# RG-LRU mixer of a two-layer trunk: another tile order, 1+a on ScalarE and GpSimd, and two interleaved output tiles

## The chip, the cores and the metric

The kernel runs on one core of one Trainium2 chip. The metric is the device time of one execution in microseconds. A profile of one execution lies beside it; its span goes from the first to the last instruction.

## What is computed

A trunk of two residual layers on x of 512 positions by 1024 channels, float32. Layer 0 mixes with pooling and block-sparse attention, layer 1 with a gated linear recurrence (RG-LRU); a gated convolutional FFN follows each. Only the mixer of layer 1 and the way out of it are touched here:

```python
def rglru_mixer(h, w_in, conv_w, conv_b, w_a, b_a, w_x, b_x, lam, w_out):   # h = rms_norm(x)
    gate, xr = jnp.split(h @ w_in, 2, axis=-1)                  # 1280 channels each: 10 tiles of 128
    xr = causal_dwconv(xr, conv_w, conv_b)                      # 4 taps
    r = sigmoid(xb @ w_a + b_a)                                 # xb: xr in 10 blocks of 128 channels
    i = sigmoid(xb @ w_x + b_x)
    a = exp(-RG_C * r * softplus(-lam))
    b = sqrt(1 - a**2) * (i * xr)
    hs = scan over positions of  hs[t] = a[t] * hs[t-1] + b[t]
    return (gelu(gate) * hs) @ w_out                            # added to x, then norm and FFN
```

## The kernel before, in words

Channels lie on the 128 partitions, the 512 positions along the free axis. A float32 product is made of three TensorE matmuls in fp32r (`mm3`): weights and activations are each split into a high and a low part, and high x high, high x low and low x high are summed in PSUM. The high part of an activation is a cast on ScalarE, the low part a subtraction on VectorE (`split_of`). Weights come by SyncE's DMA queue into three raw buffers; `convert` casts a chunk on ScalarE (line 195, `whi`), subtracts on VectorE (line 196, `wlo`) and keeps four converted chunks; `wnext` asks for the chunk in use and three ahead. The chunks of 512 columns for the gates have one buffer of their own in this stage (`shi`, `slo`).

The mixer's work for ten tiles is listed letter by letter in `RG_ORDER` (line 64):

- x: 24 matmuls of a branch tile (`xr`), times the norm's row factor (line 786, `z`), first tap on ScalarE (789), three taps on VectorE (791), high and low part (796, 797, `xrs`). The first x also asks for the norm's factor: two matmuls (`bc`), a root and a reciprocal (283).
- p: the tile's two gate products, three matmuls each (`gp`), a sigmoid for each (809), then i times xr on GpSimd (813) and a tanh for the root's argument (815).
- g: 24 matmuls of a gate tile (`gt`) and the row factor (756).
- e, q: exponentials (760) and roots (765) of all tiles so far, each with its own activation table.
- s: one VectorE instruction makes (1+a) times the root (770), GpSimd multiplies by i times xr (771), VectorE scans (772).
- o, y: gelu of the gate tile (775); product with the scan's result (779) and its split (230, 231), which gives `yh`, `yl`.

The scheduler orders each engine's instructions when the kernel is built, those traced first ahead of others that are ready; TensorE's matmuls are tied into the order of the letters within this stage (`in_order`, with `pe["on"]` true), and each engine works through its own list in order. After the letters, `down((5, 5), ...)` makes eight output tiles (`dn`), one after another, each from ten tiles of `yh`, `yl` (30 matmuls) with two weight chunks of 640 columns; the sum is added to `X[d]` (312) and goes into the next norm.

Of the kernel before, what the change touches and what calls it, by code (L numbers as in the profile page):

```python
# [17 lines left out]
P = 128  # L18
# [20 lines left out]
    _n += _w  # L39
NPA = _n  # L40

# Order of the first mixer: u/f = pooled projection now / as filler between attention steps, c = centre a window sum,
# v = value projection, m = split a pooled tile, a = attention.
MIX_ORDER = "u3 c3 u2 v m m f1 f0 a".split()
# Fillers of the attention loop: u = next projection group, m = split, p = pooled product, o = output product.
FILL_ORDER = "uuuuuuuuuuuuuuuuupmmpopp"
POOL_ORDER = (3, 2, 1, 0)
FILL_RATES = [float(c) for c in "1.6 1.95 1.45".split()]
# [8 lines left out]
CENTRE_AT = 5  # L57
V_BANKS = ("mm", "mm", "s", "av")
WARM = 20
# Order of the RG-LRU: x = branch tile, p = its gate products, g = gate tile, e = exps, q = roots, s = scan, o = gelu,  # L60
# y = output tile.
RG_ORDER = []
_c = dict.fromkeys("xpgeqsoy", 0)
for _kind in "xxgxpxpqxpgpgpeqsxsxxsssopyooxpxypygpgpqesssoosygsogyyogoyyggooyy":
    RG_ORDER.append((_kind, _c[_kind]))
    _c[_kind] += 1
RAW, WB, AHEAD = 3, 4, 3
# [3 lines left out]
def tile_trunk(ctx: ExitStack, tc: tile.TileContext, xT, par, fpar, w_v, w_q, w_k, w_u, w_pool, w_po, w_ao,  # L71
# [30 lines left out]
    def MM(name):  # L102
        ring.append(ring.pop(0))
        return PS(name, ring[-1])
# [51 lines left out]
    for kind, n in RG_ORDER:  # L156
# [4 lines left out]
                chunks.append((r_ax[n // 2], 4 * P))  # L161
        elif kind == "g":
            chunks.append((r_in[n], 1024))
    for d in range(KD):
        chunks.extend([(r_out[d][:, :5 * P], 5 * P), (r_out[d][:, 5 * P:], 5 * P)])
    ffn_chunks(f1_in, f1_out)
    ready = []
    used = [0]
# [30 lines left out]
    def wnext(n, ahead=AHEAD):  # L199
        while len(ready) < min(used[0] + 1 + ahead, len(chunks)):  # L200
            convert()
        hi, lo, got = ready[used[0]]
        assert got == n
        used[0] += 1
        return hi, lo
# [17 lines left out]
    def mm3(ps, sh, sl, mh, ml, start, stop):  # L223
        mmul(ps, lhsT=sh, rhs=mh, start=start, stop=False, skip_group_check=True)
        mmul(ps, lhsT=sh, rhs=ml, start=False, stop=False, skip_group_check=True)
        mmul(ps, lhsT=sl, rhs=mh, start=False, stop=stop, skip_group_check=True)
# [69 lines left out]
            mm3(ps, wh[:, c], wl[:, c], norm.xh[k], norm.xl[k], k == 0, k == KD - 1)  # L296
        return ps

    def down(parts, yh, yl, after, cuts=None):
        nk = len(yh)  # L300
        for d in range(KD):
            w = [wnext(n * P) for n in parts]
            spans = cuts if cuts and d == KD - 1 else [slice(0, S)]
            for t in spans:
                ps = MM("dn")
                k = 0
                for n, (wh, wl) in zip(parts, w):
                    for i in range(n):
                        c = slice(i * P, (i + 1) * P)
                        mm3(ps[:, t], wh[:, c], wl[:, c], yh[k][:, t], yl[k][:, t], k == 0, k == nk - 1)  # L310
                        k += 1
                nc.vector.tensor_tensor(X[d][:, t], ps[:, t], X[d][:, t], op=ALU.add)  # L312
                if len(spans) > 1:
                    after(d, t)
            if len(spans) == 1:
                after(d)

# [1 line left out]
    phase("mix0", qka=20, pm=4, hn=5, bias=1, lg=4)  # L319
    psum("ps0", mm=3, s=2, tr=2, av=1)  # L320
    warm = onesr.bitcast(BF16)
# [356 lines left out]
        g()  # L678
    ring[:] = ["mm", "s", "mm", "s", "mm", "av"]

# [1 line left out]
    def ffn(layer, norm, after, cuts=None):  # L682
        def conv(m):
            c0 = (layer * 2 * NF + m) * 4
# [30 lines left out]
    n1 = Norm("nm1")  # L715
    ffn(0, nf, n1.tile_done)

# [1 line left out]
    phase("mix1", z=2, a=3, xrs=6, i=2, h=10, gz=6, shi=1, slo=1, yy=20)  # L719
    lam = prm[:, PC["lam"]:PC["lam"] + RB]  # L720
    sc = [cst.tile([P, RB], F32, name=f"sc{i}") for i in range(5)]
# [30 lines left out]
    for kind, n in RG_ORDER:  # L752
        if kind == "g":
            ps = up_tile(n1, "gt")
            GZ[n] = T("gz")
            nc.vector.tensor_tensor(GZ[n], ps, n1.bc, op=ALU.mult)
            continue
        if kind == "e":
            while exped < len(HS):
                tabled("exp", nc.scalar.activation(R[exped], R[exped], AF.Exp, scale=c8[:, exped:exped + 1]))  # L760
                exped += 1
            continue
        if kind == "q":
            while rooted < len(HS):
                tabled("sqrt", nc.scalar.activation(HS[rooted], HS[rooted], AF.Sqrt))
                rooted += 1
            continue
        if kind == "s":
            h = HS[n]
            nc.vector.scalar_tensor_tensor(h, R[n], 1.0, h, op0=ALU.add, op1=ALU.mult)  # L770
            nc.gpsimd.tensor_tensor(h, h, BB[n], op=ALU.mult)
            nc.vector.tensor_tensor_scan(h, R[n], h, 0.0, op0=ALU.mult, op1=ALU.add)  # L772
            continue
        if kind == "o":
            tabled("gelu", nc.scalar.activation(GZ[n], GZ[n], AF.Gelu_apprx_tanh))
            continue
        if kind == "y":
            z = GZ[n]
            nc.vector.tensor_tensor(z, HS[n], z, op=ALU.mult)
            yh[n], yl[n] = split_of(z, None, T("yy", F32R), T("yy", F32R))  # L780
            continue
        if kind == "x":
            ps = up_tile(n1, "xr")
            bc = n1.bc
            z = T("z")
            nc.vector.tensor_tensor(z, ps, bc, op=ALU.mult)
            cw = [pc("rcw", 4 * n + i) for i in range(4)]
            a = T("a")
            nc.scalar.activation(a, z, AF.Identity, scale=cw[3], bias=pc("rcb", n))
            for sh in range(1, 4):  # L790
                ins = nc.vector.scalar_tensor_tensor(a[:, sh:], z[:, :S - sh], cw[3 - sh], a[:, sh:], op0=ALU.mult,  # L791
                                                     op1=ALU.add)
                if sh == 1:
                    behind(ins, now["conv"])
            hi, lo = T("xrs", F32R), T("xrs", F32R)
            nc.scalar.copy(hi, a)
            now["conv"] = nc.vector.tensor_sub(lo, a, f(hi))
            XC[n] = (a, hi, lo)
            continue
        a, xh, xl = XC[n]  # L800
        if n % 2 == 0:
            gwh, gwl = wnext(4 * P)
        gt = []
        for s in range(2):
            c = slice((2 * (n % 2) + s) * P, (2 * (n % 2) + s + 1) * P)
            gp = PS("gp", "tr")
            mm3(gp, gwh[:, c], gwl[:, c], xh, xl, True, True)
            o = T("yy" if s == 0 else "i")
            tabled("sig", nc.scalar.activation(o, gp, AF.Sigmoid, bias=pc("ba" if s == 0 else "bx", n)))
            gt.append(o)  # L810
        R[n] = gt[0]
        BB[n] = T("yy")
        nc.gpsimd.tensor_tensor(BB[n], gt[1], a, op=ALU.mult)
        HS[n] = T("h")
        tabled("sig", nc.scalar.activation(HS[n], R[n], AF.Tanh, scale=c4[:, n:n + 1]))
    pe["on"] = False
    nf1 = Norm("nf1")
    down((5, 5), yh, yl, nf1.tile_done)
    phase("ffn1", z=4, a=4, gg=2, y=2, yy=30)

    def store(d, t=slice(0, S)):
# [74 lines left out]
```

## Time and profile before

| what | value |
|---|---|
| median of 3 runs | 1108.43 us (1108.22 to 1109.06) |
| span of the profiled execution | 1106.8 us |
| TensorE busy | 1091.4 us (99%) |
| VectorE, ScalarE, GpSimd busy | 726.8, 514.6, 89.7 us |
| granted TensorE clock, mean | 0.997 |
| mixer of layer 1, first branch matmul to the last output tile | 553.5 to 743.8 us |

The execution takes 1.6 us more than its span in the median of the runs. A matmul of 512 columns shows 0.39 us, but the next one starts 0.227 us after it: 24 of them take 5.44 us in the chain of work. An instruction on VectorE of 128x512 shows 0.68 us while the next starts 0.60 us after it. The time between brackets in a timeline row is the engine's idle time before it and what ended it.

### The profile page before, as it was taken

To read this page: it belongs to the slowest core of one execution; us is meant where nothing else is said; L and a number is where in the kernel's file an instruction comes from. 1 tells how busy PE (TensorE), PEld (TensorE's weight loads), DVE (VectorE), ACT (ScalarE), POOL (GpSimd) and SP (SyncE) were. 2 spreads that over 40 slices of the span, in tenths; PEclk is the share of its full clock that TensorE was granted. 3 is DMA by queue.
4 is the path that set the end of the run, shared out by engine and by line. 5 is a ranking of instruction groups with operands and counts; after the bars stand their busy time and mean duration, and the time that the engine had idled before them with its cause. 6 is when DMAs were issued, how large, how long until landed. Compare 5 with 4: busy or idle time off the path is not lost.

```text
span 1106.8 us, 12775 instructions
## 1 busy us (share of the span) xinstructions
PE 1091.4 (99%) x4895; PEld 893.2 (81%) x4895; DVE 726.8 (66%) x1013; ACT 514.6 (46%) x749; POOL 89.7 (8%) x70
## 2 busy tenths in 40 slices
PE   8999999999999999999999899999999999999998
PEld 6887778888888888888888687788888888888887
DVE  7777867877753477764486979448777435777631
ACT  6556656544432344444458695444444323444320
POOL 4030002100000000000202323120000000000000
PEclk9999999999999999999999999999999999999999
DMA  6332112222223322223332131342322243332241
GB/s 223 129 95 87 58 39 71 102 95 96 72 82 111 117 96 98 94 73 91 113 113 105 48 101 48 99 136 95 102 97 78 79 119 116 96 95 84 72 137 51
DMA packets 35261, 105.40 MB, mean 95 GB/s; under 512 B 4096, under 2 KB 4992, under 8 KB 35200
## 3 DMA queue, kind: packets, MB, share of 16 engines
q1 hardware_dynamic: 34416, 103.48, 28.7%
q10 hardware_dynamic: 784, 1.11, 0.4%
q8 instruction: 38, 0.62, 0.2%
q14 instruction: 23, 0.19, 0.1%
HBM read 101.43 MB, written 2.10 MB: 94 GB/s over the span
## 4 chain that ended last, share of the span: by engine, by line
PE 90%; DVE 6%; ACT 2%; issue 1%; DMA 0%; POOL 0%; SPq 0%; DVEq 0%; POOLq 0%; ACTq 0%
PE up L218 43%; PE dn L218 26%; PE tk L218 5%; PE xr L218 2%; PE gt L218 2%; PE po L218 2%; PE u L218 2%; PE ao L218 2%; DVE h L772 1%; PE s L218 1%; DVE wlo L196 1%; PE tr L221 1%; PE gp L218 1%; DVE a L791 1%; DVE h L770 1%
## 5 line engine op out<-in xcount | busy, mean ns | idle before, releaser
L195 ACT CAST whi<-wraw 128x1024 fp32r<-128x1024 f32 (+3 forms) x225 | 202.5, 904 | 281.0 <-PE dn L218 154.2
L196 DVE TENSOR_TENSOR wlo<-wraw,whi 128x1024 fp32r<-128x1024 f32 (+3 forms) x225 | 238.9, 1065 | 114.2 <-ACT whi L195 111.6
L218 PE MATMUL up<-xl,whi 128*128 128x512 f32 x704 | 274.0, 389 | 0.0
L218 PE MATMUL up<-xh,whi 128*128 128x512 f32 x704 | 273.9, 389 | 0.0
L218 PE MATMUL up<-xh,wlo 128*128 128x512 f32 x704 | 273.9, 389 | 0.0
L218 PE MATMUL dn<-yy,whi 128*128 128x512 f32 (+1 forms) x886 | 269.2, 386 | 2.4 <-ACT yy L230 2.0
L218 PEld LDWEIGHTS dn<-yy,whi 128*128 128x128 f32 x886 | 165.8, 189 | 36.9 <-ACT yy L230 2.8
L218 PE MATMUL dn<-yy,wlo 128*128 128x512 f32 (+1 forms) x443 | 170.7, 385 | 0.0
L218 PEld LDWEIGHTS up<-xl,whi 128*128 128x128 f32 x704 | 132.2, 188 | 27.9 <-DVE xl L234 0.5
L218 PEld LDWEIGHTS up<-xh,whi 128*128 128x128 f32 x704 | 132.2, 188 | 27.4
L218 PEld LDWEIGHTS up<-xh,wlo 128*128 128x128 f32 x704 | 132.2, 188 | 27.2
L693 DVE SCALAR_TENSOR_TENSOR a<-z,fprm,a 128x510 f32<-128x510 f32 (+1 forms) x176 | 131.1, 748 | 4.2 <-ACT a L691 1.1
L689 DVE TENSOR_TENSOR z<-up,rbc 128x512 f32<-128x512 f32 x88 | 60.5, 688 | 89.1 <-PE up L218 89.1
L218 PEld LDWEIGHTS dn<-yy,wlo 128*128 128x128 f32 x443 | 83.6, 189 | 16.4
L260 POOL TENSOR_TENSOR ss<-ss,sq 128x512 f32<-128x512 f32 x28 | 41.3, 1475 | 494.1 <-ACT sq L259 493.6
L230 ACT CAST yy<-y 128x512 fp32r<-128x512 f32 x44 | 27.3, 621 | 112.1 <-DVE y L707 112.1
L312 DVE TENSOR_TENSOR x<-dn,x 128x512 f32<-128x512 f32 (+1 forms) x41 | 27.8, 679 | 73.9 <-PE dn L218 73.9
L691 ACT ACTIVATE a<-z,fprm 128x512 f32<-128x512 f32 x88 | 71.4, 814 | 3.8 <-DVE z L689 3.2
L704 ACT ACTIVATE gg<-a 128x512 f32<-128x512 f32 x44 | 27.8, 632 | 81.1 <-DVE a L693 81.0
L231 DVE TENSOR_TENSOR yy<-y,yy 128x512 fp32r<-128x512 f32 x44 | 30.5, 692 | 28.9 <-ACT yy L230 28.9
L218 PE MATMUL tk<-wlo,xh 128*128 128x512 f32 x96 | 37.7, 392 | 1.9 <-DVE wlo L196 1.9
L218 PE MATMUL tk<-whi,xh 128*128 128x512 f32 x96 | 37.9, 400 | 1.2 <-ACT whi L195 1.2
(177 smaller groups left out, 1229.5 us busy)
## 6 DMA issues: line engine op xcount, KB each, us to landing
wraw<-in_dram SPq DMA_DIRECT2D x131, 512.0 KB, 3.3
wraw<-in_dram SPq DMA_DIRECT2D x48, 320.0 KB, 2.8
wraw<-in_dram SPq DMA_DIRECT2D x32, 384.0 KB, 3.0
x<-in_dram SPq DMA_DIRECT2D x8, 256.0 KB, 5.9
out_dram<-x SPq DMA_DIRECT2D x7, 256.0 KB, 2.0
wraw<-in_dram SPq DMA_DIRECT2D x6, 256.0 KB, 2.7
qka<-qka ACTq DMA_DIRECT2D x8, 128.0 KB, 2.6
wraw<-in_dram SPq DMA_DIRECT2D x4, 128.0 KB, 3.8
```

The source lines that it names most:

```text
L195: nc.scalar.copy(hi[:, c], raw[:, c])
L196: nc.vector.tensor_tensor(lo[:, c], raw[:, c], f(hi[:, c]), op=ALU.subtract)
L218: in_order(nc.tensor.matmul(*a, **k))
L221: in_order(nc.tensor.transpose(*a))
L230: nc.scalar.copy(hi, src)
L231: nc.vector.tensor_sub(lo, src, f(hi))
L260: nc.gpsimd.tensor_tensor(self.ss, self.ss, sq, op=ALU.add)
L312: nc.vector.tensor_tensor(X[d][:, t], ps[:, t], X[d][:, t], op=ALU.add)
L689: nc.vector.tensor_tensor(z, ps, bc, op=ALU.mult)
L691: nc.scalar.activation(a, z, AF.Identity, scale=cw[2], bias=cw[3])
L693: nc.vector.scalar_tensor_tensor(a[:, sh:], z[:, :S - sh], w, a[:, sh:], op0=ALU.mult, op1=ALU.add)
L704: nc.scalar.activation(gg, g, AF.Gelu_apprx_tanh)
```

## The change

`RG_ORDER` gets another string: four p stand among the first x, the first g comes after the first e and q, and later letters alternate. In step s the VectorE instruction of line 770 goes; ScalarE writes 1+a into a tile of the pool `i` (two buffers, shared with the gate i), GpSimd multiplies it into i times xr, GpSimd multiplies the root by that, and the scan follows. In `down`, the mixer's call sets `paired`: the first two output tiles take their first five inputs one after the other, then their last five; the weight chunks are ordered to suit. Comment lines go.

```diff
-for _kind in "xxgxpxpqxpgpgpeqsxsxxsssopyooxpxypygpgpqesssoosygsogyyogoyyggooyy":
+for _kind in "xxpxpxpxpxpeqgssxpssgsxpooyygxpoygxpoygpeqgssoygssoygsoygoygoyoy":
...
-    for d in range(KD):
-        chunks.extend([(r_out[d][:, :5 * P], 5 * P), (r_out[d][:, 5 * P:], 5 * P)])
+    halves = [slice(0, 5 * P), slice(5 * P, 10 * P)]
+    chunks += [(r_out[d][:, c], 5 * P) for c in halves for d in range(2)]
+    chunks += [(r_out[d][:, c], 5 * P) for d in range(2, KD) for c in halves]
...
-    def down(parts, yh, yl, after, cuts=None):
+    def down(parts, yh, yl, after, cuts=None, paired=False):
         nk = len(yh)
-        for d in range(KD):
+        if paired:
+            ps = [MM("dn") for _ in range(2)]
+            k0 = 0
+            for n in parts:
+                for d in range(2):
+                    wh, wl = wnext(n * P)
+                    for i in range(n):
+                        c = slice(i * P, (i + 1) * P)
+                        k = k0 + i
+                        mm3(ps[d], wh[:, c], wl[:, c], yh[k], yl[k], k == 0, k == nk - 1)
+                k0 += n
+            for d in range(2):
+                nc.vector.tensor_tensor(X[d], ps[d], X[d], op=ALU.add)
+                after(d)
+        for d in range(2 if paired else 0, KD):
...
             h = HS[n]
-            nc.vector.scalar_tensor_tensor(h, R[n], 1.0, h, op0=ALU.add, op1=ALU.mult)
+            up1 = T("i")
+            nc.scalar.activation(up1, R[n], AF.Identity, bias=ones)
+            nc.gpsimd.tensor_tensor(BB[n], up1, BB[n], op=ALU.mult)
             nc.gpsimd.tensor_tensor(h, h, BB[n], op=ALU.mult)
             nc.vector.tensor_tensor_scan(h, R[n], h, 0.0, op0=ALU.mult, op1=ALU.add)
...
-    down((5, 5), yh, yl, nf1.tile_done)
+    down((5, 5), yh, yl, nf1.tile_done, paired=True)
```

## Rows read from the trace of the kernel before

**Rows 1.** Page, busy time of the engines, share of the span, instructions.

```profile
PE 1091.4 (99%) x4895; PEld 893.2 (81%) x4895; DVE 726.8 (66%) x1013; ACT 514.6 (46%) x749; POOL 89.7 (8%) x70
```

**Rows 2.** Stretches: start:end, length, busy us (instructions) by engine, clock, DMA share, GB/s.

```profile
553.50:604.20 50.70, 50.70 (x226) 41.85 (x225) 39.23 (x44) 32.21 (x44) 6.91 (x5) 1.00 0.31 108
604.20:655.30 51.10, 47.27 (x199) 38.07 (x198) 46.37 (x52) 39.60 (x55) 17.22 (x10) 0.97 0.23 77
655.30:683.90 28.60, 27.36 (x122) 22.32 (x121) 21.79 (x24) 18.29 (x27) 10.54 (x6) 1.00 0.15 42
683.90:698.00 14.10, 11.67 (x41) 8.52 (x40) 11.41 (x17) 7.55 (x13) 0.00 (x0) 0.88 0.39 114
```

**Rows 3.** TensorE's waits from 550 to 760: total us, times, longest.

```profile
PE gp L218 <- ACT xrs L796: 3.2, 1, 3.2
PE dn L218 <- ACT yy L230: 2.0, 1, 2.0
PE gt L218 <- DVE wlo L196: 1.2, 1, 1.2
```

**Rows 4.** Chain of work: start us, length us, what.

```profile
564.90 5.44 PE gt L218 x24
...
575.78 1.36 PE gp L218 x6
```

**Rows 5.** VectorE's timeline at the mixer's start: start us, length us, instruction.

```profile
561.00 3.34 DVE L283 RECIPROCAL rbc<-ss 128x512 f32<-128x512 f32 x1
...
565.80 1.22 DVE L196 TENSOR_TENSOR wlo<-wraw,whi 128x1024 fp32r<-128x1024 f32 x1
566.94 2.31 DVE L791 SCALAR_TENSOR_TENSOR a<-z,prm,a 128x511 f32<-128x511 f32 x3
570.00 0.69 DVE L797 TENSOR_TENSOR xrs<-a,xrs 128x512 fp32r<-128x512 f32 x1 [0.74 <-ACT xrs L796]
```

**Rows 6.** ScalarE's timeline at the mixer's start.

```profile
565.67 1.52 ACT L789 ACTIVATE a<-z,prm 128x512 f32<-128x512 f32 x2
569.35 0.62 ACT L796 CAST xrs<-a 128x512 fp32r<-128x512 f32 x1 [2.16 <-DVE a L791]
```

**Rows 7.** Stretch right after TensorE's longest wait, columns as in Rows 2.

```profile
625.00:630.00 5.00, 5.00 (x16) 3.91 (x17) 5.00 (x7) 3.68 (x6) 0.00 (x0) 0.66 0.20 52
```

**Rows 8.** VectorE's timeline during the second five scans.

```profile
667.74 0.66 DVE L770 SCALAR_TENSOR_TENSOR h<-yy,h 128x512 f32<-128x512 f32 x1
668.32 1.21 DVE L772 TENSOR_TENSOR_SCAN h<-yy,h 128x512 f32<-128x512 f32 x1
669.46 1.71 DVE L770 SCALAR_TENSOR_TENSOR h<-yy,h 128x512 f32<-128x512 f32 x1
```

**Rows 9.** GpSimd's timeline: one product early, one during the second five scans.

```profile
580.00 1.29 POOL L813 TENSOR_TENSOR yy<-i,a 128x512 f32<-128x512 f32 x1 [22.48 <-ACT i L809]
...
668.54 2.07 POOL L771 TENSOR_TENSOR h<-h,yy 128x512 f32<-128x512 f32 x1 [1.81 <-DVE h L770]
```

**Rows 10.** VectorE's groups from 604.2 to 655.3: busy us, mean ns, idle before.

```profile
L196 DVE TENSOR_TENSOR wlo<-wraw,whi 128x1024 fp32r<-128x1024 f32 x7 | 9.5, 1369 | 0.2 <-ACT whi L195 0.2
...
L779 DVE TENSOR_TENSOR gz<-h,gz 128x512 f32<-128x512 f32 x3 | 2.0, 677 | 0.0
L756 DVE TENSOR_TENSOR gz<-gt,rbc 128x512 f32<-128x512 f32 x2 | 1.4, 678 | 0.0
```

**Rows 11.** Stretch of the second five scans and their products, columns as in Rows 2.

```profile
663.00:693.80 30.80, 27.16 (x116) 21.11 (x114) 28.19 (x34) 16.23 (x25) 9.08 (x5) 1.00 0.17 52
```

**Rows 12.** ScalarE's timeline after the last gate products.

```profile
656.23 0.71 ACT L815 ACTIVATE h<-yy,c 128x512 f32<-128x512 f32 x1
656.96 1.28 ACT L765 ACT_TABLE_LOAD   x1
658.26 2.71 ACT L765 ACTIVATE h<-h 128x512 f32<-128x512 f32 x5
660.98 1.28 ACT L760 ACT_TABLE_LOAD   x1
662.27 3.18 ACT L760 ACTIVATE yy<-yy,c 128x512 f32<-128x512 f32 x5
```

**Rows 13.** VectorE's timeline, low part of the last product y.

```profile
693.08 0.69 DVE L231 TENSOR_TENSOR yy<-gz,yy 128x512 fp32r<-128x512 f32 x1 [0.68 <-ACT yy L230]
```

## The prediction

> **What bounds the kernel now.** I read the page first, for the engine that is full: TensorE is busy for 99% of the span [rows 1], so a change pays only where it takes away time in which TensorE waits or runs slowly, or costs by making such time. Then the stretches of the mixer of layer 1, to see how much of that there is. Twenty-four matmuls take 5.44 us and the six of a gate pair 1.36 us [rows 4], so one matmul is 5.44/24 = 0.227 us. The first stretch holds eight 24-matmul tiles, five gate pairs and the two norm matmuls: 8 x 5.44 + 5 x 1.36 + 0.48 = 50.8 us in 50.7: nothing is lost. The second holds seven tiles and five pairs, 44.9 us in 51.1: 6.2 lost. The third holds five gate tiles, 27.2 in 28.6: 1.4 lost. The fourth holds 41 matmuls, 9.3 in 14.1: 4.8 lost [rows 2]. In all 12.4 us; no order of this stage can give back more.
>
> The waits say which instruction ends the loss: gate products wait 3.2 us for a high part of a branch tile, an output tile 2.0 us for the high part of a product y, a gate tile 1.2 us for a weight's low part [rows 3]. The rest of the 12.4 is slow running: after the longest wait the granted clock was 0.66 in 625 to 630, that is part of the stretch at 1.2 GHz and part at 2.4 [rows 7]. All three releasers hang on VectorE, or on ScalarE fed by VectorE. VectorE is busy for 46.4 of 51.1 us in the second stretch [rows 2] and 28.2 of 30.8 us from the second block of scans to the last y [rows 11]. So the mixer's bound is VectorE's queue, and how it stands against TensorE's order.
>
> VectorE's busy time hides a second user. A scan alone takes 1.21 us and line 770 alone 0.66; the next line 770, started at 669.46, took 1.71, ending at 671.17 [rows 8]. GpSimd's product began at 668.54, took 2.07 where it needs 1.29 alone, and ended at 670.61 [rows 9], 0.56 us before VectorE's ended. GpSimd stood still while the scan ran, and VectorE while GpSimd ran: with operands in SBUF the two take turns, and a GpSimd product costs VectorE up to 1.29 us, 1.05 in this pair (1.71 - 0.66).
>
> **The change part by part.** *The opening.* Before, the first gate products start at 575.78, after a gate tile and a third branch tile that fill 564.90 to 575.78 [rows 4]. Now "xxp" puts them at 564.90, and the matmul order is tied to the letters. Their input is the first branch tile's split: reciprocal until 564.34, first tap at 565.67, a weight's low part at 565.80, three taps from 566.94 to 569.25, cast from 569.35 to 569.97, low part from 570.00 to about 570.6 [rows 5, 6]. Nothing in the change makes this chain earlier: the reciprocal follows the last output tile of the FFN, and converted weight chunks are released by the same matmuls as before. So TensorE stands still from 564.90 to about 570.0 (5.1 us), makes one matmul and waits for the low part (0.5 us more). If the taps went ahead of the weight's low part (1.13 us) it would be 4.0 and 0.5. Then the clock: from the 3.2 us wait I take its price as the 6.2 us lost there less 3.2 and less about 1.5 us of second waits and slow gate products: 1.5 us; here 0.5 to 1.7. I take 5.6 + 1.2 = 6.8 us (bounds 4.5 to 7.5).
>
> *The pairs p1 to p4.* Each waits for a split whose tile ended one pair and one tile earlier: 1.36 + 5.44 = 6.8 us. The chain is row factor 0.6, first tap 0.8, three taps 2.3, cast 0.7, low part 0.6, and a GpSimd product in between 1.29 [rows 5, 6, 9]: 6.3 us, 7.4 if a weight's low part stands in front. So 0 to 0.6 us for each of three: 1 us in all (0 to 3).
>
> *From p4 to p9.* TensorE has now nine tiles and five pairs here, 9 x 5.44 + 5 x 1.36 = 55.8 us. Against the second stretch of before, VectorE has two more weight chunks (+2 x 1.2), two more gate tiles and one more y (about +1.3 each) [rows 10], and five line-770 instructions fewer (-5 x 0.66 [rows 8]): 46.4 + 5.0 - 3.3 = 48.1 us. GpSimd has five products more; a product adds between 0.8 us (if part of it falls into VectorE's idle time; an estimate from the 46.4 us, which are 8 us above what its 52 instructions take undisturbed, for ten products) and 1.29: 4.0 to 6.5. With the 4.7 us of idle of that stretch [rows 2] it comes to 56.8 to 59.2, against 55.8. x6 to x8 each have a gate tile between them and their p, so the lag shows at p9 alone. I take 2 us (0 to 6). ScalarE's ten additions of 0.76 each (its nearest row is the first tap, two in 1.52 [rows 6]) and one more table load of 1.28 [rows 12] find room, since it is busy for 39.6 of 51.1 us [rows 2]; without that room they would add up to 5 us here, because casts queue behind them.
>
> *After p9.* Count from the end of p9, 655.3 before. Before, tanh ends 1.6 us after it, and roots and exponentials with two loads end 10.1 us after it, while line 770 starts already at 663.0, +7.7 [rows 11, 12]. Now the addition comes behind both blocks on ScalarE: +10.1 + 0.8 = +10.9 until GpSimd can begin, and two GpSimd products stand ahead of each scan. VectorE's work from there: the 30.8 us of before [rows 11], less 5 x 0.66, less one y that now comes before p9 (1.3), plus five GpSimd products (4.0 to 6.5): 30.2 to 32.7. The last y is thus ready at +41.1 to +43.6; before it was at 693.8 [rows 13], +38.5. What TensorE can do meanwhile: five gate tiles, 27.2, and then in the paired order twice five inputs (30 matmuls, 6.8 us) and four more (2.7): it needs the last y at +36.7. One tile alone would need it at 27.2 + 9 x 0.68 = +33.3; the pairing gives 3.4 us. Left: 4.4 to 6.9 us. I take the low end and a clock loss of 1.0, 5.4 us (0 to 9; nothing if additions get ahead of roots, and TensorE fills the wait with a third output tile).
>
> The sum: 6.8 + 1 + 2 + 5.4 = 15.2 us lost in place of 12.4: +2.8 us on the profiled execution, 1106.8 + 2.8 = 1109.6 of span, and with the 1.6 us between span and median 1111.2 us. Moved DMAs are costed at nothing: SyncE's queue brings the same chunks at 108 GB/s and less in these stretches [rows 2], in the order of use; if a load came late it would cost one chunk's wait, as 1.2 us in [rows 3].
>
> By the Trainium skill, "SBUF — State Buffer", section "SBUF: two separate sides", the shared pair of ports is locked against GpSimd only by a VectorE instruction with two SBUF inputs or one in a two-port mode. No row here has a GpSimd product beside a multiplication out of PSUM, so no run shows it yet; by that rule the row factors of lines 756 and 786 would run beside GpSimd, which is the third rival.
>
> **The rivals.** *Faster, through slack.* The order gathers the recurrence's first half early and leaves gate tiles, which are cheap for VectorE (0.68 us each [rows 10] against some 4.5 for a branch tile), as filler. If that keeps every later split ahead of TensorE and the last y comes by +36.7, only the opening is lost: 6.8, perhaps 8 with a small wait. Then 12.4 - 8 to 12.4 - 6.8 = 4.4 to 5.6 us faster, about 1103.5. For it: p5 to p8 have 12 us of slack. Against it: VectorE and GpSimd together have more to do than before in both later stretches, and were full. It decides at +36.7 us after p9.
>
> *Worse, through two buffers.* The additions share two buffers with the gate i. If ScalarE stands at an addition whose buffer GpSimd still reads, casts queue behind it, and with them matmuls. With every GpSimd product at 1.29 and the queue's waits the upper bounds hold: 7 + 2 + 5 + 9 = 23 lost, +10.6: about 1119. For it: two GpSimd products for each scan; against: ScalarE has idle time.
>
> *Row factors beside GpSimd.* Nine row factors of 0.6 between p4 and p9 and four after p9 run while GpSimd works. That takes the 2 us of the middle away and 2.4 of the end: 15.2 - 4.4 = 10.8 lost, 1.6 us less than before: 1106.8. It needs them to fall together with products, which two lists in order don't promise.
>
> **How the numbers follow.** About 0.2% (2.2 us) is what a measurement of this kernel can tell from no change. My forecast, 1111.2 (own range 1108.5 to 1117), gets 0.50; faster through slack 0.25; row factors beside GpSimd 0.15; two buffers 0.10. Faster: 0.25. Slower: 0.10 and 0.42 of the forecast's 0.50. Same: the 0.15 and the forecast's lower edge, 0.08: 0.23. The range takes in the fast case and the slow one but for their tails: 1103 to 1119.
>
> **What would show it.** Right: TensorE idle for some 5 us before the first gate products, released by the first branch tile's split, with a clock below 1 soon after; small waits or none at p5 to p8; GpSimd twice as busy in the scans, VectorE instructions there over 1.6 us; the first scan of the second half 13 us after p9 instead of 10.2, and an output-tile matmul waiting for a late y. Wrong: the first pair not waiting (then the 6.8 goes, and it is faster), TensorE without a wait after p9, or waits for ScalarE's additions in the middle.

## The result, and the profile after

| | before | after |
|---|---|---|
| median | 1108.45 us (1108.22 to 1109.06) | 1126.49 us (1126.0 to 1126.88) |
| span of the profiled execution | 1106.8 us | 1124.4 us |
| granted TensorE clock, mean | 0.997 | 0.989 |

The ratio is 1.016 (95% interval 1.0145 to 1.0174): 18.0 us slower. The prediction was 1111.2 (1103 to 1119). It had the direction and missed the size: the loss is over six times the forecast's 2.8 us.

In after, most lines of before stand one line later up to the function `down`, and 15 to 17 lines later in the mixer: matmuls are L219, a weight's low part L197, scans L789, the two GpSimd products L787 and L788, the addition 1+a L786, the taps L808, the split of a branch tile L813 and L814. In the other kernels the numbers shift by a few lines; the names of the tiles tell which instruction it is.

The page of after, busy time of the engines, which answers to [rows 1]:

```profile
PE 1098.2 (98%) x4895; PEld 896.8 (80%) x4895; DVE 726.5 (65%) x1003; ACT 522.4 (46%) x760; POOL 102.6 (9%) x80
```

TensorE has the same 4895 matmuls and no longer fills the span. VectorE lost ten instructions and is as busy as before (726.5 against 726.8); GpSimd gained ten products and 12.9 us.

The stretches of after, cut where p4, p9 and the mixer's last output tile end (start:end, length, busy us and instructions of PE, PEld, DVE, ACT, POOL, then clock, DMA share, GB/s); the first two answer to the first two of [rows 2], and the last two lines are short stretches behind two waits, as [rows 7]:

```profile
553.50:603.60 50.10, 44.33 (x178) 34.47 (x177) 36.90 (x40) 27.64 (x38) 7.01 (x5) 0.93 0.25 85
603.60:672.30 68.70, 59.55 (x248) 47.48 (x247) 52.89 (x53) 49.11 (x67) 23.37 (x15) 0.93 0.25 78
672.30:761.40 89.10, 84.03 (x362) 69.06 (x361) 49.48 (x58) 48.52 (x71) 25.39 (x17) 0.96 0.30 86
570.00:575.00 5.00, 4.21 (x9) 3.13 (x10) 3.45 (x6) 3.81 (x6) 0.00 (x0) 0.50 0.12 48
699.40:712.00 12.60, 7.53 (x24) 5.74 (x23) 12.59 (x15) 4.89 (x8) 4.83 (x3) 0.73 0.21 57
```

With the prediction's 0.227 us a matmul (24-matmul tile 5.44, gate pair 1.36, the norm's two 0.48) the work needs 39.9, 55.8 and 81.6 us in these three stretches: six tiles and five pairs; nine tiles and five pairs; five gate tiles and eight output tiles of 30 matmuls. So 10.2, 12.9 and 7.5 us are lost, 30.6 in all (each to some 0.2 us). Cut at the same events, before loses 0, 6.2 and 6.9 (743.76 - 655.3 - 81.6): 13.1. The difference, 17.5, is within 0.1 us what the span grew by, 17.6. These three numbers are the measure for every experiment below.

TensorE's waits of after, 550 to 775 (engine, line, waited for: total us, times, longest), against [rows 3]:

```profile
PE gp L219 <- ACT xrs L813: 8.4, 3, 5.1
PE gt L219 <- DVE wlo L197: 5.4, 1, 5.4
PE dn L219 <- DVE wlo L197: 5.1, 1, 5.1
PE gp L219 <- DVE xrs L814: 0.9, 4, 0.2
```

The long ones in TensorE's timeline (in brackets the wait before the instruction and what ended it): the opening, two in the middle, one among the output tiles.

```profile
570.79 1.52 PE L219 MATMUL gp<-xrs,whi 128*128 128x512 f32 x2 [5.10 <-ACT xrs L813]
...
629.30 0.50 PE L219 MATMUL gp<-xrs,shi 128*128 128x512 f32 x1 [2.45 <-ACT xrs L813]
...
638.03 0.80 PE L219 MATMUL gt<-xh,wlo 128*128 128x512 f32 x1 [5.44 <-DVE wlo L197]
...
705.05 0.80 PE L219 MATMUL dn<-yy,wlo 128*128 128x512 f32 x1 [5.07 <-DVE wlo L197]
```

The first was forecast (5.1 us). The two longest of the others wait for the low part of a weight, which has nothing to do with the recurrence but for standing in VectorE's list. Its timeline in the first block of scans shows behind what:

```profile
618.32 2.30 DVE L789 TENSOR_TENSOR_SCAN h<-yy,h 128x512 f32<-128x512 f32 x1 [2.99 <-POOL h L788]
...
624.41 4.18 DVE L808 SCALAR_TENSOR_TENSOR a<-z,prm,a 128x511 f32<-128x511 f32 x3
...
633.57 2.27 DVE L789 TENSOR_TENSOR_SCAN h<-yy,h 128x512 f32<-128x512 f32 x1 [2.47 <-POOL h L788]
635.77 2.21 DVE L197 TENSOR_TENSOR wlo<-wraw,whi 128x1024 fp32r<-128x1024 f32 x1
```

and GpSimd's timeline beside it:

```profile
629.95 2.24 POOL L787 TENSOR_TENSOR yy<-i,yy 128x512 f32<-128x512 f32 x1 [2.68 <-ACT i L786]
632.26 1.27 POOL L788 TENSOR_TENSOR h<-h,yy 128x512 f32<-128x512 f32 x1
633.50 1.26 POOL L787 TENSOR_TENSOR yy<-i,yy 128x512 f32<-128x512 f32 x1
634.84 2.06 POOL L788 TENSOR_TENSOR h<-h,yy 128x512 f32<-128x512 f32 x1
```

Read the two together from 632.26. The product of L788 ends at 633.53, and the scan that needs it starts at 633.57, after VectorE had stood idle for 2.47 us. The next GpSimd product (633.50 to 634.76) falls on the scan, which takes 2.27 us in place of 1.21 [rows 8]. Behind it the weight's low part starts at 635.77 and meets the next product (634.84 to 636.90): 2.21 us in place of 1.22 [rows 5]. It ends at 637.98, and TensorE goes on at 638.03 after 5.44 us. The low part had no other work in front of it than a scan; the scan had two GpSimd products in front of it. The three taps at 624.41 show the same stretching: 4.18 us, against 2.31 [rows 5].

### The profile page after: what moved, and what is told of

It is laid out like the page before. It is cut to its first block, busy times and chain, and to the rows that moved or that the text cites. A ratio compares the mean times of both kernels' runs of the same rounds, so it can differ in the third digit from the quotient of the medians.

```text
span 1124.4 us, 12782 instructions
## 1 busy us (share of the span) xinstructions
PE 1098.2 (98%) x4895; PEld 896.8 (80%) x4895; DVE 726.5 (65%) x1003; ACT 522.4 (46%) x760; POOL 102.6 (9%) x80
## 4 chain that ended last, share of the span: by engine, by line
PE 88%; DVE 4%; ACT 4%; issue 1%; POOL 1%; DMA 0%; SPq 0%; ACTq 0%; POOLq 0%; DVEq 0%
PE up L219 43%; PE dn L219 26%; PE tk L219 5%; PE xr L219 2%; PE u L219 2%; PE po L219 2%; PE ao L219 2%; DVE a L808 2%; PE s L219 1%; PE gt L219 1%; DVE wlo L197 1%; PE tr L222 1%; PE av L219 1%; PE gp L219 1%; POOL yy L787 1%
## 5 line engine op out<-in xcount | busy, mean ns | idle before, releaser
L196 ACT CAST whi<-wraw 128x1024 fp32r<-128x1024 f32 (+4 forms) x226 | 203.2, 903 | 279.7 <-PE dn L219 153.8
L197 DVE TENSOR_TENSOR wlo<-wraw,whi 128x1024 fp32r<-128x1024 f32 (+4 forms) x226 | 240.3, 1067 | 109.8 <-ACT whi L196 107.2
L219 PE MATMUL up<-xl,whi 128*128 128x512 f32 x704 | 274.0, 389 | 0.0
L219 PE MATMUL up<-xh,whi 128*128 128x512 f32 x704 | 273.9, 389 | 0.0
L219 PE MATMUL up<-xh,wlo 128*128 128x512 f32 x704 | 273.9, 389 | 0.0
L219 PE MATMUL dn<-yy,whi 128*128 128x512 f32 (+1 forms) x886 | 268.6, 385 | 0.0
L219 PEld LDWEIGHTS dn<-yy,whi 128*128 128x128 f32 x886 | 166.1, 189 | 33.3
L219 PE MATMUL dn<-yy,wlo 128*128 128x512 f32 (+1 forms) x443 | 171.1, 386 | 5.1 <-DVE wlo L197 5.1
L219 PEld LDWEIGHTS up<-xl,whi 128*128 128x128 f32 x704 | 132.2, 188 | 28.1 <-DVE xl L235 0.5
L219 PEld LDWEIGHTS up<-xh,wlo 128*128 128x128 f32 x704 | 132.2, 188 | 27.3
L219 PEld LDWEIGHTS up<-xh,whi 128*128 128x128 f32 x704 | 132.2, 188 | 27.2
L219 PEld LDWEIGHTS dn<-yy,wlo 128*128 128x128 f32 x443 | 83.8, 189 | 22.0 <-DVE wlo L197 5.5
L219 PE MATMUL tk<-whi,xh 128*128 128x512 f32 x96 | 38.8, 410 | 0.6 <-ACT whi L196 0.6
L219 PE MATMUL tk<-wlo,xh 128*128 128x512 f32 x96 | 38.1, 397 | 0.9 <-DVE wlo L197 0.9
```

Source lines behind the costliest of these rows:

```text
L196: nc.scalar.copy(hi[:, c], raw[:, c])
L197: nc.vector.tensor_tensor(lo[:, c], raw[:, c], f(hi[:, c]), op=ALU.subtract)
L219: in_order(nc.tensor.matmul(*a, **k))
```

## The experiments

Each experiment is one edit of before or of after. "Lost" means the three numbers above: opening to the end of p4, to the end of p9, to the end of the mixer. A difference with a sign is against runs of before taken beside it (medians 1109.31, 1109.20 and 1108.73 us in three sets of runs); "less than after" compares medians of different sets. The lost numbers are those of the one profiled execution, which lies up to 1.7 us from its kernel's median. Six kernels give every engine the same list up to the end of p4 (after, and below the letters alone, 1+a back on VectorE, the product on VectorE, the scans set apart and the scans late), and they lose 8.8 to 10.2 us there; so 1 us or so between two lost numbers says nothing.

### Each part of the change alone

Three kernels take one part each into before. The order of the letters:

```diff
-for _kind in "xxgxpxpqxpgpgpeqsxsxxsssopyooxpxypygpgpqesssoosygsogyyogoyyggooyy":
+for _kind in "xxpxpxpxpxpeqgssxpssgsxpooyygxpoygxpoygpeqgssoygssoygsoygoygoyoy":
```

> The kernel before with the new string of letters alone; 1+a stays on VectorE, output tiles one after another. Theory A (the two-product step is what makes scans stand at the head of VectorE's list, with weights' low parts behind them): only the opening's loss of about 9 us is new, and the rest loses about as before, so 1113 to 1118. Theory B (the letters alone make the waits): 1122 or more, with the 5.4 us wait of a gate tile for a weight's low part still there.

Measured: 1122.81, ratio 1.0124 (1.0109 to 1.0139), +13.5 us; lost 10.2, 10.4, 7.5. The time is theory B's, but the 5.4 us wait that B names is not there: the gate products wait for splits. Its TensorE waits:

```profile
PE gp L218 <- ACT xrs L810: 9.9, 3, 5.1
PE dn L218 <- ACT yy L230: 3.5, 3, 2.0
PE gp L218 <- DVE xrs L811: 2.4, 4, 1.8
```

The 1+a step alone:

```diff
-            nc.vector.scalar_tensor_tensor(h, R[n], 1.0, h, op0=ALU.add, op1=ALU.mult)
+            up1 = T("i")
+            nc.scalar.activation(up1, R[n], AF.Identity, bias=ones)
+            nc.gpsimd.tensor_tensor(BB[n], up1, BB[n], op=ALU.mult)
```

> The kernel before with 1+a on ScalarE and the second product on GpSimd, nothing else. Theory A: 1114 to 1122, with TensorE's waits for weights' low parts or splits during both blocks of scans. Theory B: 1108 to 1111, since the old letters hide the step.

Measured: 1119.69, ratio 1.0091 (1.0074 to 1.0108), +10.4 us; lost 0, 13.2, 11.1, as theory A had it. Its TensorE waits:

```profile
PE gt L218 <- DVE wlo L196: 7.1, 1, 7.1
PE gp L218 <- DVE xrs L813: 5.2, 2, 4.9
PE gp L218 <- ACT xrs L812: 4.7, 1, 4.7
```

The interleaved output tiles alone:

```diff
+    halves = [slice(0, 5 * P), slice(5 * P, 10 * P)]
+    chunks += [(r_out[d][:, c], 5 * P) for c in halves for d in range(2)]
+    chunks += [(r_out[d][:, c], 5 * P) for d in range(2, KD) for c in halves]
...
-    down((5, 5), yh, yl, nf1.tile_done)
+    down((5, 5), yh, yl, nf1.tile_done, paired=True)
```

> The kernel before with the first two output tiles interleaved, nothing else. By the terms of the prediction the last y is needed 3.4 us later, which takes away the 2.5 us of waits at the end and the slow clock behind them: 1104 to 1106 by both theories. If the pairing only moves the wait: 1108.

Measured: 1103.58, ratio 0.9948 (0.9933 to 0.9963), -5.7 us, a little better than expected; lost 0, 6.2, 1.8. From the end of p9 on, only one wait is left, and the granted clock is 1.00. The stretch (the mixer's last matmul ends 0.72 us behind it) and its wait:

```profile
655.30:738.00 82.70, 81.45 (x359) 66.97 (x358) 53.02 (x65) 44.90 (x66) 18.84 (x12) 1.00 0.32 96
```

```profile
PE gt L219 <- DVE wlo L197: 1.2, 1, 1.2
```

Two of the three cost, by different waits, and the third, which the prediction valued at 3.4 us, pays 5.7: with the 2.0 us wait for a y [rows 3] the slow running behind it (clock 0.88 in the fourth of [rows 2]) goes, too. The sum 13.5 + 10.4 - 5.7 = 18.2 meets the measured 18.0, but not because the parts are independent, as a kernel below with letters and interleaving, but without the step, shows: it is 10.6 us slower than before, so interleaving is worth 2.9 beside the new letters, and the step costs another 7.4, which makes the 18.0. Two deviations of some 3 us cancel.

### The opening

The first gate products one branch tile later, in after; everything else as it is:

```diff
-for _kind in "xxpxpxpxpxpeqgssxpssgsxpooyygxpoygxpoygpeqgssoygssoygsoygoygoyoy":
+for _kind in "xxxpxpxpxppeqgssxpssgsxpooyygxpoygxpoygpeqgssoygssoygsoygoygoyoy":
```

> The changed kernel with one branch tile moved ahead of the first gate products (letters xxxpxpxpxpp in place of xxpxpxpxpxp); the rest as changed. If the opening's loss (about 9 us in the trace after) reaches the end: 1117 to 1119. If VectorE's later backlog sets the end and swallows it: 1123 to 1126.

Measured: 1120.93, ratio 1.0105 (1.009 to 1.012), 5.6 us less than after; lost 2.9, 14.8, 8.2. The 5.1 us wait is gone, and the opening has back 7.3 us. Of these some 2 are lost again in the middle and 0.7 at the end: at the scans TensorE waits 3.1 and 5.1 us, as in after (2.45 and 5.44). Neither expectation was met; the time lies between them. So the opening's loss is real, and a part of it seems only to move, though that part is little more than two executions can differ by.

### What in the step costs

After, with 1+a back on VectorE (letters and interleaving stay):

```diff
-            up1 = T("i")
-            nc.scalar.activation(up1, R[n], AF.Identity, bias=ones)
-            nc.gpsimd.tensor_tensor(BB[n], up1, BB[n], op=ALU.mult)
+            nc.vector.scalar_tensor_tensor(h, R[n], 1.0, h, op0=ALU.add, op1=ALU.mult)
```

> The changed kernel with 1+a back on VectorE: new letters and interleaved output tiles. If the parts add up (letters +13.5 us, step +10.4, pairing -5.7 against before): 1116 to 1118. If the step costs only because the new letters set scans in bursts: 1109 to 1113.

Measured: 1119.84, ratio 1.0098 (1.0083 to 1.0113), +10.6 us; lost 9.9, 10.2, 4.1. That is above both expectations. Without the step, the opening's loss stays whole, and 10.2 of the middle's 12.9 us stay as well.

After, with the addition on ScalarE kept and only the product moved from GpSimd to VectorE:

```diff
-            nc.gpsimd.tensor_tensor(BB[n], up1, BB[n], op=ALU.mult)
+            nc.vector.tensor_tensor(BB[n], up1, BB[n], op=ALU.mult)
```

> The changed kernel, 1+a still on ScalarE behind the roots, but its product with i times xr on VectorE (0.6 us) in place of GpSimd (1.29 us): one GpSimd product for a scan, as before the change. If the second GpSimd product makes the step's cost: 1116 to 1120, near the kernel with 1+a on VectorE. If the addition's place in ScalarE's list makes it: 1124 to 1127.

Measured: 1118.72, ratio 1.0092 (1.0077 to 1.0107), 7.8 us less than after; lost 8.8, 8.2, 5.6, as expected if the second GpSimd product makes the cost. The second product is better on VectorE than on GpSimd, though VectorE is the fuller engine. With one GpSimd product for each scan, the addition on ScalarE makes no loss: this kernel is not told apart from the one with 1+a on VectorE (runs of 1118.06 to 1120.82 against 1119.05 to 1120.29). So beside the new letters the step costs nothing once its product leaves GpSimd. Whether the addition's place in ScalarE's list adds to the price when the product is on GpSimd is not shown: no run has two GpSimd products without an addition in front. GpSimd's timeline of this kernel shows the last three products of the first block standing apart: GpSimd waits for VectorE before each.

```profile
624.23 1.29 POOL L788 TENSOR_TENSOR h<-h,yy 128x512 f32<-128x512 f32 x1 [3.97 <-DVE yy L787]
626.75 2.12 POOL L788 TENSOR_TENSOR h<-h,yy 128x512 f32<-128x512 f32 x1 [1.23 <-DVE yy L787]
632.35 2.21 POOL L788 TENSOR_TENSOR h<-h,yy 128x512 f32<-128x512 f32 x1 [3.48 <-DVE yy L787]
```

### Is it the place of the scans, or their amount?

If the waits came only from the letters' order, the scans could be put where TensorE has filler. Three attempts on after. First, five scans set apart from one another:

```diff
-for _kind in "xxpxpxpxpxpeqgssxpssgsxpooyygxpoygxpoygpeqgssoygssoygsoygoygoyoy":
+for _kind in "xxpxpxpxpxpeqgsxpsgsxpsoygsoyxpoygxpoygpeqgssoygssoygsoygoygoyoy":
```

> The changed kernel with the first five scans set apart, one behind each tile (letters e q g s x p s g s x p s o y g s o y x p in place of e q g s s x p s s g s x p o o y y g x p); TensorE's order, the opening and everything after p9 as changed. Theory B' (the burst: scans of four tiles ahead of a branch tile's taps and of weights' low parts on VectorE): the 12.9 us lost between p4 and p9 shrink to 4 to 7, so 1117 to 1121. Theory of amounts (VectorE and GpSimd together are too full between p4 and p9): 1125 to 1128, since not one instruction goes.

Measured: 1123.81, ratio 1.0136 (1.012 to 1.0153), 2.7 us less than after; lost 9.2, 10.6, 7.9. This lies between the two theories: the middle shrank by 2.3 us and not to 4 to 7. The waits moved on to later gate products:

```profile
639.64 0.50 PE L219 MATMUL gp<-xrs,shi 128*128 128x512 f32 x1 [1.05 <-ACT xrs L813]
...
644.61 0.80 PE L219 MATMUL gp<-xrs,shi 128*128 128x512 f32 x1 [4.46 <-DVE xrs L814]
```

Second, the first five scans late, and each scan held in VectorE's list behind the last split and the last weight's low part traced before it, so that neither of the two old waits can come back:

```diff
-for _kind in "xxpxpxpxpxpeqgssxpssgsxpooyygxpoygxpoygpeqgssoygssoygsoygoygoyoy":
+for _kind in "xxpxpxpxpxpeqgxpgxpsssssooyygxpoygxpoygpeqgssoygssoygsoygoygoyoy":
...
-    raws = []
+    raws, low = [], [None]
...
-            nc.vector.tensor_tensor(lo[:, c], raw[:, c], f(hi[:, c]), op=ALU.subtract)
+            low[0] = nc.vector.tensor_tensor(lo[:, c], raw[:, c], f(hi[:, c]), op=ALU.subtract)
...
-            nc.vector.tensor_tensor_scan(h, R[n], h, 0.0, op0=ALU.mult, op1=ALU.add)
+            behind(behind(nc.vector.tensor_tensor_scan(h, R[n], h, 0.0, op0=ALU.mult, op1=ALU.add), now["conv"]), low[0])
```

> The changed kernel with the first five scans' letters behind the eighth branch tile's gate tile (e q g x p g x p s s s s s o o y y g x p) and each scan held, in VectorE's list, behind the last branch split and weight's low part traced before it. TensorE's list is the same, and no instruction is added or removed. Theory of list order (scans that wait for GpSimd stand ahead of splits and low parts that TensorE needs): the waits at the seventh gate pair and at the next gate tile (2.5 + 5.4 us and the slow clock behind) go, 1117 to 1120. Theory of amounts: the waits move to the next pairs, 1124 to 1127.

Measured: 1124.75, ratio 1.0147 (1.0132 to 1.0162), 1.7 us less than after; lost 9.1, 12.1, 7.3. That is what the theory of amounts had. Both old waits of the middle are gone, and a longer one stands at the next split:

```profile
656.82 0.80 PE L219 MATMUL gp<-xrs,shi 128*128 128x512 f32 x1 [7.02 <-ACT xrs L813]
```

VectorE's timeline of this kernel says why:

```profile
633.29 2.31 DVE L789 TENSOR_TENSOR_SCAN h<-yy,h 128x512 f32<-128x512 f32 x1
636.72 2.30 DVE L789 TENSOR_TENSOR_SCAN h<-yy,h 128x512 f32<-128x512 f32 x1 [1.12 <-POOL h L788]
638.94 0.66 DVE L771 TENSOR_TENSOR gz<-gt,rbc 128x512 f32<-128x512 f32 x1
641.40 4.46 DVE L789 TENSOR_TENSOR_SCAN h<-yy,h 128x512 f32<-128x512 f32 x2 [1.80 <-POOL h L788]
...
648.02 1.21 DVE L789 TENSOR_TENSOR_SCAN h<-yy,h 128x512 f32<-128x512 f32 x1
...
650.87 0.68 DVE L803 TENSOR_TENSOR z<-xr,rbc 128x512 f32<-128x512 f32 x1
```

Five scans occupy VectorE from 633.29 to 649.2, 16 us for 6 us of scans, and the row factor z, with which the next tile's split begins, starts at 650.87. Third, this, holds and all, together with the later opening:

```diff
+for _kind in "xxxpxpxpxppeqgxpgxpsssssooyygxpoygxpoygpeqgssoygssoygsoygoygoyoy":
```

> The changed kernel with both: one branch tile moved ahead of the first gate products, and the first five scans late and held. If opening and list order are two separate losses, they add up: 1112 to 1115; what is left over the kernel before is GpSimd's second products and the end. If one hides behind the other: 1117 to 1121.

Measured: 1117.96, ratio 1.0083 (1.0066 to 1.01); lost 3.5, 12.1, 8.0. That is 6.8 us below the second attempt, so the opening's gain comes through here, and the middle is again at 12; the two gains of the first expectation don't add up, since the late scans had none to give. With two GpSimd products for each scan, six orders lose between p4 and p9 12.9 (after), 13.2 (the order of before), 14.8, 10.6, 12.1 and 12.1 us. With one, the middle loses 6.2 us in the order of before, 10.4, 10.2 and 8.2 in the new one, and 5.6 and 9.0 in two further orders below. So both count: the order makes some 4 us in either group, and no order tried with two products loses less than the worst with one.

### The same question in the kernel that gained

Before, with the interleaved output tiles, and then with the letters of the first scans changed. Letter x ahead of the first s:

```diff
-for _kind in "xxgxpxpqxpgpgpeqsxsxxsssopyooxpxypygpgpqesssoosygsogyyogoyyggooyy":
+for _kind in "xxgxpxpqxpgpgpeqxsxsxsssopyooxpxypygpgpqesssoosygsogyyogoyyggooyy":
```

> The kernel before with the interleaved output tiles, and with the sixth branch tile's letter ahead of the first scan (e q x s x s x in place of e q s x s x x). The taps of that tile then come ahead of the first scans on VectorE; TensorE's own order is unchanged. If scans ahead of the taps make the 3.2 us wait at that tile's gate products and the slow clock behind it (5.8 us lost): 1098 to 1101. If the backlog only moves: 1103 to 1106.

Measured: 1104.33, ratio 0.996 (0.9945 to 0.9975). The scheduler gave every engine the same list as with interleaving alone, so this says nothing on the letters; it is a repeat, 0.75 us from the first. With the holds of the scans from above, the letters do change VectorE's list:

> The kernel before with the interleaved output tiles, the sixth branch tile's letter ahead of the first scan, and each scan held behind the last branch split and weight's low part traced before it. List order: the 3.2 us wait at that tile's gate products and its slow clock (5.8 us) shrink, 1098 to 1101. Amounts: 1103 to 1105.

Measured: 1103.02, ratio 0.995 (0.9935 to 0.9965), the fastest time here and 5.7 us below before, though not told apart from interleaving alone (1103.58): the expectation from amounts. The 3.2 us wait of [rows 3] has become several shorter ones, and the middle still loses 5.6 us:

```profile
PE gp L219 <- ACT yy L824: 2.1, 2, 1.7
PE gt L219 <- DVE wlo L197: 1.5, 1, 1.5
PE gp L219 <- ACT xrs L811: 0.9, 1, 0.9
```

And with all five first scans late, held likewise:

```diff
+for _kind in "xxgxpxpqxpgpgpeqxxxpsssssoyooxpxypygpgpqesssoosygsogyyogoyyggooyy":
```

> The kernel before with the interleaved output tiles, and all five first scans' letters behind the sixth gate pair (e q x x x p s s s s s o y o o x), held as in the run before. List order: 1097 to 1101, the wait at the sixth pair gone. Amounts: the wait turns up at the seventh or eighth pair instead, 1103 to 1106.

Measured: 1105.66, ratio 0.9974 (0.9964 to 0.9984); the middle loses 9.0 us, again as expected from amounts, with one wait of 4.93 us at a later gate product, behind five scans in one piece (VectorE from 631.25 to 637.9). The row names a sigmoid of ScalarE as what ended the wait; ahead of it in ScalarE's list stood the cast of a y, which had waited 3.29 us for VectorE to come out of the scans.

```profile
640.81 1.22 PE L219 MATMUL gp<-xrs,shi 128*128 128x512 f32 x2 [4.93 <-ACT yy L824]
```

Even with one GpSimd product for each scan, neither of these two places keeps the first five scans from stopping TensorE; in one piece they do it longer.

## Why the prediction was right or wrong

*What bounds the kernel: right.* The mixer's bound is VectorE's list against TensorE's order, and GpSimd's products take turns with VectorE. Every new wait of over 1 us but the opening's ends behind a scan.

*The opening, 6.8 forecast (4.5 to 7.5), 8.8 measured at the end of the third branch tile: the mechanism right, the size off.* The wait was 5.10 us for the 5.1 foreseen, by the split foreseen. The mis-sized term is what follows. The granted clock was 0.50 in 570 to 575, that is 1.2 GHz throughout; the chain of after shows the gate pair at 3.23 us in place of 1.36 and the branch tile behind it at 6.46 in place of 5.44:

```profile
570.79 3.23 PE gp L219 x6
574.02 6.46 PE xr L219 x23
```

That is 2.9 us where the low part's wait and the clock had 1.7. Part of it is chance: the six kernels with the same lists up to here all wait 5.10 us, and then lose 1.9 to 3.1 us by the end of the third branch tile. The other 0.8 came ahead of the wait: TensorE reached it at 565.69 instead of 564.90. Most of that, 0.6, lies at the norm's two matmuls and is not the change's: the second kernel with interleaving alone shows it too, with the letters of before, and the kernel with the second product on VectorE, which has the new letters, does not.

*The pairs p1 to p4: right* (1 forecast, 10.2 - 8.8 = 1.4 measured).

*From p4 to p9, 2 us forecast (0 to 6), 12.9 measured: the step that failed.* Of the 15.4 us by which the loss in after, 30.6, exceeds the forecast's 15.2, 10.9 arise here. The sum there was VectorE's busy time, 52.1 to 54.5, plus the idle time of before, 4.7. The busy time was right: 52.89. The idle time was not carried over: 68.70 - 52.89 = 15.8 us. GpSimd's products ended 5.5 us of it, TensorE itself, late with a branch tile, 5.4, and ScalarE's first tap 3.2 (VectorE's waits of after, 603.6 to 672.3; total us, times, longest):

```profile
DVE h L789 <- POOL h L788: 5.5, 2, 3.0
DVE z L803 <- PE xr L219: 5.4, 2, 4.7
DVE a L808 <- ACT a L806: 3.2, 4, 1.5
```

The step asked whether 57 to 59 us of VectorE's work and idle time fit into 56 us, and took the gate tiles between x6 to x8 and their p as cover, so that a lag would show at p9 alone. At p9 TensorE waited 0.80 us; it waited 2.45 at p6, the pair of the seventh branch tile, and 5.44 in the gate tile behind it. The slack of p5 to p8 holds on the average, and the scans come in a block. The first block's products take GpSimd from 615.62 to 636.90, 21 us, with two products of 1.3 to 2.2 us for each scan; the same five scans of before had one, from 608.64 to 620.04. VectorE's list is in order, so a split or a weight's low part that stands behind a scan waits for both products, and the 6.8 us from one pair to the next are spent.

Most of this loss doesn't need the second product. With the new letters and one GpSimd product for each scan the stretch loses 10.4 us (letters alone), 10.2 (1+a back on VectorE) and 8.2 (the product on VectorE), so the step had failed for the letters already. Beside the new letters the second product adds 2.5 to 4.7 us here; beside the letters of before it adds 7.0 (6.2 to 13.2). The group of the ten scans of after, whole mixer (busy us, mean ns, idle before), puts the second product's part into one line:

```profile
L789 DVE TENSOR_TENSOR_SCAN h<-yy,h 128x512 f32<-128x512 f32 x10 | 18.6, 1862 | 12.2 <-POOL h L788 12.2
```

The same ten scans of before, and the instructions of line 770 that the change removed:

```profile
L772 DVE TENSOR_TENSOR_SCAN h<-yy,h 128x512 f32<-128x512 f32 x10 | 15.3, 1536 | 2.4 <-POOL h L771 2.4
L770 DVE SCALAR_TENSOR_TENSOR h<-yy,h 128x512 f32<-128x512 f32 x10 | 9.7, 999 | 4.0 <-ACT yy L760 4.0
```

Removed: 9.7 us of work and 4.0 of waiting. Added on the scans alone: 3.3 us of work and 9.8 of waiting for GpSimd. VectorE's busy time on the page fell by 0.3 us only, so the rest of the removed work came back elsewhere: 3.6 us of it in the three taps of the ten tiles (30.8 us against 27.2), of which 2.7 show with the letters alone (29.9).

With the letters alone the longest wait here is one of 4.02 us for the same split, of the seventh branch tile, whose taps start at 626.10, behind three of the five scans; that the letters cost by the place of the scans is a reading of these rows and not shown, for with two products moving the scans brought little back. Letters and step together give 12.9, not the 17.4 of their sum: they spend the same slack.

*After p9, 5.4 forecast (0 to 9), 7.5 measured: the sum close, the wait another.* The first scan came 15.3 us after p9 (687.60), for 13 forecast, and the low part of the last y was ready at 715.90, +43.6, the upper edge of the 41.1 to 43.6:

```profile
715.21 0.69 DVE L232 TENSOR_TENSOR yy<-gz,yy 128x512 fp32r<-128x512 f32 x1 [0.74 <-ACT yy L231]
```

But TensorE did not wait for any y: the list of waits above has no row for one, and the forecast's sign of an output tile waiting for a late y did not come. TensorE stopped at 699.98, some 9 us before the point at which the forecast has it need the last y (+36.7), at the third matmul of the first output tile: the low part of that weight stood behind the scan of 700.97 and began at 703.18, which gave 5.07 us and a clock of 0.73 up to 712. That the sums come so close is luck.

```profile
700.97 2.29 DVE L789 TENSOR_TENSOR_SCAN h<-yy,h 128x512 f32<-128x512 f32 x1
703.18 1.82 DVE L197 TENSOR_TENSOR wlo<-wraw,whi 128x640 fp32r<-128x640 f32 x1
```

*The interleaving* was worth 5.7 us beside the letters of before, not 3.4: the clock that came back with the wait was left out of its term. Beside the new letters it was worth 2.9.

*Loads* were costed at nothing, rightly: in the mixer of after no wait of TensorE, VectorE or ScalarE is put down to a load. With the letters alone one cast of a weight waited 3.13 us for a load, until 627.80, but the chain of work from 620.98 to 633.9 runs through VectorE and GpSimd and not through that cast. The 108 GB/s given as the most in [rows 2] is 114 in its fourth line, which changes nothing.

*The rivals.* Faster through slack fell with the middle. Worse through two buffers gave 1119, nearest to the truth by its time and not by its mechanism: in the mixer of after ScalarE never waited for a product of GpSimd to free a buffer. With the step alone it did, twice, 1.8 us in all. Once an addition of after did stand in ScalarE's list behind a cast that waited 7.44 us for VectorE's taps, and GpSimd waited 2.68 us for it (the product of 629.95 above); that is the place in the list and not a wait for a buffer. The row factors beside GpSimd run as that rival says: VectorE's line 771 out of PSUM took 0.68 us while a GpSimd product ran from 694.18 to 695.71. In all traces together 18 row factors run beside a GpSimd product for 0.45 us or more, and none takes over 0.69.

```profile
694.48 0.68 DVE L771 TENSOR_TENSOR gz<-gt,rbc 128x512 f32<-128x512 f32 x1
```

```profile
694.18 1.53 POOL L787 TENSOR_TENSOR yy<-i,yy 128x512 f32<-128x512 f32 x1 [3.20 <-ACT i L786]
```

By the Trainium skill, "SBUF — State Buffer", section "SBUF: two separate sides", of VectorE's instructions those with two SBUF inputs, or in a two-port mode, lock the pair of ports against GpSimd. These two rows agree, and the scans at 2.3 us beside products show the other half. What this saved in after was not measured; the middle lost more and not less.

*Left open.* How much of the second product's price is VectorE being held while GpSimd runs, and how much is the scan's longer chain. Both are in the rows (stretched instructions, and idle time ended by GpSimd); no run separates them. Nor does a run show what in the new letters costs the 4.2 us of the middle that they add to before.

## What to carry to other kernels

Before moving work to an idle engine, ask what in an in-order list will wait for its result: here 9.7 us came off VectorE, and 9.8 us more of waiting for GpSimd took their place. Check the added chain against the time from one consumer to the next at the place where the operations bunch together, not busy time against the length of a stage; and for each waiting instruction ask what stands behind it in its list, even if it belongs to another part of the work. When several edits come together, cost each of them apart, for here the one that gained 5.7 us was hidden under two that cost 24.

## What the runs showed of the hardware

A wait of 5.10 us cost TensorE another 1.9 to 3.1 us in six executions with the same lists up to there, a short second wait included; in after it was 2.9, with the granted clock at 0.50 in 570 to 575. A 128x512 product on GpSimd took 1.29 us alone [rows 9] and in after up to 2.24 beside VectorE, and a scan of 1.21 us took up to 2.3 beside a product; but a VectorE product reading PSUM kept its 0.68.
